# Query and key tiles turned by VectorE in 32x32 blocks instead of TensorE, in a two-layer streaming trunk

## The chip, the cores and the metric

The kernel runs on one NeuronCore of a Trainium2 chip. The metric is the device time of one execution in microseconds (us), median over the runs; lower is better. TensorE ran at its full granted clock in the profile of before.

## What is computed

`x` is 2048 tokens of 1024 channels. Layer A is a gated pooling mixer; layer B is stick-breaking attention with 16 heads of 64 channels against keys and values that are computed once from the output of layer A. The change lies where queries and keys are made:

```python
kv_in = rms_norm(x, kv_norm)
k_all, v_all = jnp.split(kv_in @ w_kv, 2, axis=-1)
k_sh = rms_norm(split_heads(k_all), k_norm)      # over the 64 channels of a head
v_sh = split_heads(v_all)
h = rms_norm(x, b_norm[j])
q, z = jnp.split(h @ b_w_in[j], 2, axis=-1)
q = rms_norm(split_heads(q), b_q_norm[j])
...
logits = jnp.einsum('bhtd,bhsd->bhts', q[:, :, t0:L], k[:, :, :L]) * SB_SCALE
```

The attention wants queries and keys with channels on the partitions; the norm over a head's channels is taken with tokens on the partitions. So each q and k tile has to be turned once.

## The kernel before

Every product is done in split precision: each operand is a pair (high part rounded to fp32r, low part the remainder), and three matmuls of 128x128 by 128x512 stand for one product.

The first half of the program, the dense stage, goes over four chunks `s` of 512 tokens. A chunk has 22 steps, written as a list: eight for the mixer (`run_z`, `run_u`), four for its output (`run_o`), four for the gate (`run_g`), and six token-major ones (`run_kvq`): q, k and v, each in two halves `b` of 512 channels (8 heads). A `run_kvq` step does two passes (`j0` = 0 and 2); a pass makes two tiles `j` of 128 tokens by 512 channels with 48 matmuls, in which the activations `ck["x2"]` (channels by tokens) are the stationary operand and the weights move. Tile `j` holds the tokens `128*j` to `128*j+127`.

For q and k, ScalarE takes a tile out of PSUM and scales it by the token's rsqrt (`keyed`: `qs`, then its square), VectorE sums the squares per head, GpSimd makes the rsqrt `rq`, and VectorE multiplies (`normed`: `qn`). When all four tiles of a half are there, four closures `finish(m)`, one for each pair of heads, are put on the list `lag`. They are issued at the end of the next step's first pass, after its last matmul group:

```python
while j0 == 0 and kt == KT - 1 and lag:
    lag.pop(0)()
```

Each `finish(m)` has TensorE turn four 128x128 blocks into PSUM (`pst`, two buffers), ScalarE write the high part of `hl` and VectorE the low part (for q both times the joint gain `gqk`), and the SP queue store `hl` (512 KB) to DRAM as `qd` or `kd`. `hl` has four buffers of a kind (`t4`) that weight repacking and the v tiles use too.

Weights for the coming steps are fetched by the SP queue (`fetch`) and made into pairs by ScalarE and VectorE (`convert`, L148 and L149 for q, k, v). The SP queue issues in program order (`queue` pins it), and so do the matmul stream and the operations marked `keep_in_program_order`; the rest is placed by a scheduler when the program is built. Each engine then works through its own row of instructions in order.

The second half is the attention: 16 heads by 4 query chunks by the key chunks below, with the z projection and the whole output stage of layer B as filler between the tiles. It reads `qd`, `kd`, `vd` back from DRAM and uses the per-token rsqrt `r2s` once more in `gate_z`.

Of the kernel before, what the change touches and what calls it, by code (L numbers as in the profile page):

```python
# [9 lines left out]
F32 = mybir.dt.float32  # L10
# [5 lines left out]
P = 128  # L16
# [19 lines left out]
def trunk_kernel(ctx, tc, x, xt, pt0, wut, cols, heads, zin, grp, aout, agate, aple,  # L36
# [22 lines left out]
    gqk = cp.tile([P, 1], F32, name="gqk")  # L59
    r2all = cp.tile([P, NSUB, 4], F32, name="r2all")  # L60
    r2s = [r2all[:, s, :] for s in range(NSUB)]

# [4 lines left out]
    qd = [[dram.tile([P, 2, W5], F32, name=f"qd{s}_{m}") for m in range(NH // 2)] for s in range(NSUB)]  # L67
    kd = [[dram.tile([P, 2, W5], F32, name=f"kd{s}_{m}") for m in range(NH // 2)] for s in range(NSUB)]
    vd = [[dram.tile([8, P, 4, P], F32, name=f"vd{s}_{b}") for b in range(2)] for s in range(NSUB)]
    ve = [[dram.tile([4, W5], F32, name=f"ve{s}_{b}") for b in range(2)] for s in range(NSUB)]  # L70

    wod = [dram.tile([P, 2, 2, 4, P], F32, name=f"wod{o}") for o in range(KT)]
# [146 lines left out]
    with ExitStack() as st:  # L219
# [15 lines left out]
            return t2.tile([P, W5], F32, tag="tmp", name=nm, bufs=8)  # L235

        hp = st.enter_context(tc.tile_pool(name="hp", bufs=1))
        halo = [[hp.tile([P, HALO], F32, name=f"halo{o}_{i}") for i in range(2)] for o in range(KT)]
        for o in range(KT):
            V.memset(halo[o][0], 0.0)  # L240
# [251 lines left out]
        def run_u(s, g, wu):  # L492

            ck, win = chunk[s], WIN[g]
            pss2 = [dense(), dense()]
            product(pss2, wu or ck["wu"].pop(g), ck["x"], (0, P), None, second_beside(g - 1) if g and not s else ())
            if "z3" in ck:
                ck["rb"] = bcast(ck["r"], "x")
                gate_of(ck, g, ck.pop("z3"))
            for k in range(2):  # L500
                o = 2 * g + k
                ub = t2.tile([P, HALO + W5], F32, tag="ub", name="ub", bufs=2)
                G.tensor_copy(out=ub[:, 0:HALO], in_=halo[o][s % 2])
                V.tensor_tensor(out=ub[:, HALO:], in0=pss2[k], in1=ck["rb"], op=ALU.mult)
                G.tensor_copy(out=halo[o][(s + 1) % 2], in_=ub[:, W5 : W5 + HALO])
                cur, lo, sh = ub, 0, 1
                while sh < win:
                    nx = t2.tile([P, HALO + W5], F32, tag="us", name="us", bufs=2)
# [62 lines left out]
        def run_g(s, b, wg, wl):  # L571
# [21 lines left out]
            for k in range(2):  # L593
# [6 lines left out]
                    sq = na  # L600
                ck["acc"] = sq

        def run_kvq(s, kind, b, ws):
            ck = chunk[s]
            for j0 in (0, 2):
# [3 lines left out]
                pss2 = [dense(), dense()]  # L609
                for kt in range(KT):  # L610
                    for i in range(2):
                        tk = slice((j0 + i) * P, (j0 + i + 1) * P)
                        for xh, wh in ((0, 0), (1, 0), (0, 1)):
                            T.matmul(pss2[i], ck["x2"][kt][:, xh, tk], wst(ws, kt, wh, 0, W5),  # L614
                                     start=(kt == 0 and xh == 0 and wh == 0), stop=(kt == KT - 1 and wh == 1))
                    if kt == 2:
                        stored_late()
# [4 lines left out]
                if "r2" not in ck:  # L622
                    ps = turned()
                    for j in range(4):
                        T.matmul(ps[:, 0, j : j + 1], ck["acc"][:, j * P : (j + 1) * P], ones,
                                 start=True, stop=True)
                    ss = t2.tile([P, 4], F32, tag="ssx", name="ss2")
                    A.copy(out=ss, in_=ps[:, 0, 0:4])
                    rsqrt_mean(r2s[s], ss, D, t2, "x")
                    ck["r2"] = r2s[s]  # L630
                fins = [token_major(s, kind, b, j0 + i, pss2[i]) for i in range(2)]
                if kind == "v":
                    settle()
# [12 lines left out]
                    pass  # L646

        def token_major(s, kind, b, j, ps):
            tk = slice(j * P, (j + 1) * P)
            rj = chunk[s]["r2"][:, j : j + 1]  # L650
            ps8 = ps.rearrange("q (h d) -> q h d", d=HD)
            if kind == "v":

# [63 lines left out]
            return lambda: normed(s, kind, b, j, qs, rq)  # L717

        def normed(s, kind, b, j, qs, rq):
            qn = t2.tile([P, 8, HD], F32, tag="qn", name="qn", bufs=5)  # L720
            tc.keep_in_program_order(
                V.tensor_tensor(out=qn, in0=qs, in1=rq.unsqueeze(2).to_broadcast([P, 8, HD]), op=ALU.mult))
            rows = chunk[s].setdefault((kind, b), [])
            rows.append(qn)
            if j < 3:
                return

            def finish(m):
                pt = turned()
                for i in range(4):  # L730
                    ins = T.transpose(pt[:, i, :], rows[i][:, 2 * m : 2 * m + 2, :].rearrange("q h d -> q (h d)"), ident)  # L731
                    if i == 0:
                        tc.keep_in_program_order(ins)
                pt = pt.rearrange("q j t -> q (j t)")
                hl = t2.tile([P, 2, W5], F32R, tag="t4", name="hl", bufs=4)
                if kind == "k":
                    split(hl, pt, V)
                else:
                    A.activation(out=hl[:, 0], in_=pt, func=AF.Identity, scale=gqk)
                    V.scalar_tensor_tensor(out=hl[:, 1], in0=pt, scalar=gqk, in1=f(hl[:, 0]),  # L740
                                           op0=ALU.mult, op1=ALU.subtract)
                queue(out=(kd if kind == "k" else qd)[s][4 * b + m], in_=f(hl))

            for m in range(4):
                lag.append(lambda m=m: finish(m))

        def load_gains():
            nc.scalar.dma_start(out=gains, in_=cols[:, KT:])
            gs = t2.tile([P, 2], F32, tag="gs", name="gs", bufs=1)
            nc.scalar.dma_start(out=gs, in_=heads)  # L750
            return gs

        def join_gains(gs):
            V.scalar_tensor_tensor(out=gqk, in0=gs[:, 1:2], scalar=HD ** -0.5, in1=gs[:, 0:1],
                                   op0=ALU.mult, op1=ALU.mult)

        steps = []
# [582 lines left out]
```

## Time and profile before

| what | value |
|---|---|
| median of 3 runs | 2680.74 us (2680.23 to 2682.93) |
| span of the profiled execution | 2679.3 us, so 1.4 us of the median lie around it if it ran as the median did |
| TensorE matmuls | busy 2668.1 us, 13358 instructions |
| VectorE, ScalarE, GpSimd busy | 1911.5, 1397.2 and 927.7 us |
| DMA | 590.00 MB, mean 220 GB/s |
| first and last matmul of the q, k, v steps (L614) | 219.8 and 1332.6 us |

Busy times are per engine and overlap. PE is the matmul row of TensorE, PEld its weight-load row, which runs beside it: the stationary operand of a matmul is loaded while the matmul before it streams. A matmul's recorded duration is longer than the distance to the next one, because matmuls are pipelined.

### The profile page before, as it was taken

What the parts mean: (1) busy time and instruction counts of PE and PEld (TensorE: products, weight loads), DVE (VectorE), ACT (ScalarE), POOL (GpSimd) and SP (SyncE); (2) the same over time, 40 slices, a digit from 0 to 9 for tenths busy, and PEclk for the clock granted to TensorE, in tenths of its full rate; (3) what the DMA queues carried; (4) which work ended last, traced back from release to release, by engine and by line L of the source; (5) the groups of instructions that cost most, each with busy time, mean ns of one, the idle gap of its engine ahead of it and who ended that gap; (6) DMA issues with size and microseconds to landing.
All of it is one profiled execution on the core that took longest, in us unless ns stands there. A gap on an engine that the chain in (4) does not pass through costs nothing.

```text
span 2679.3 us, 39424 instructions
## 1 busy us (share of the span) xinstructions
PE 2668.1 (100%) x13358; PEld 2229.9 (83%) x13358; DVE 1911.5 (71%) x2474; ACT 1397.2 (52%) x2735; POOL 927.7 (35%) x740
## 2 busy tenths in 40 slices
PE   9999999999999999999999999999999999999999
PEld 7888888888888888888888888888888888888887
DVE  6776625665266643665399999999999998886632
ACT  6455623455135551345356666666666666665531
POOL 2675337643486434853221111122111221212220
PEclk9999999999999999999999999999999999999999
DMA  8657795567856678543679665556766677778975
GB/s 327 222 175 271 251 308 188 192 240 251 303 175 226 232 259 298 168 151 134 223 236 286 195 220 176 166 172 191 211 199 177 185 222 227 201 209 261 267 237 177
DMA packets 281366, 590.00 MB, mean 220 GB/s; under 512 B 33702, under 2 KB 67750, under 8 KB 281164
## 3 DMA queue, kind: packets, MB, share of 16 engines
q1 hardware_dynamic: 270818, 571.41, 65.3%
q0 software_dynamic: 4608, 8.39, 1.9%
q10 hardware_dynamic: 5738, 7.68, 1.0%
q8 instruction: 106, 1.74, 0.3%
q14 instruction: 96, 0.79, 0.1%
HBM read 438.40 MB, written 136.38 MB: 215 GB/s over the span
## 4 chain that ended last, share of the span: by engine, by line
PE 97%; DVE 1%; DMA 0%; issue 0%; ACT 0%; SPq 0%; ACTq 0%; DVEq 0%
PE psd L614 19%; PE psd L168 9%; PE psd L167 9%; PE psd L166 9%; PE psa L961 9%; PE psd L1023 6%; PE psd L1025 6%; PE psd L1027 6%; PE pso L974 5%; PE psl L937 5%; PE pso L973 5%; PE psl L936 5%; PE pst L731 1%; PE psdt L1023 1%; PE psdt L1025 1%; PE psdt L1027 1%
## 5 line engine op out<-in xcount | busy, mean ns | idle before, releaser
L614 PE MATMUL psd<-wpair,x 128*128 128x512 f32 x2304 | 536.8, 391 | 0.0
L948 DVE TENSOR_TENSOR_SCAN pp<-kap,pp,zeros 128x512 f32<-128x512 f32 x384 | 513.5, 1339 | 7.7 <-ACT kap L940 7.0
L964 ACT CAST at<-psa 128x512 fp32r<-128x512 f32 (+3 forms) x640 | 325.7, 523 | 348.6 <-PE psa L961 338.1
L614 PEld LDWEIGHTS psd<-wpair,x 128*128 128x128 f32 x2304 | 429.9, 188 | 87.0
L965 DVE TENSOR_TENSOR at<-psa,at 128x512 fp32r<-128x512 f32 (+3 forms) x640 | 375.1, 598 | 62.0 <-ACT at L964 57.5
L940 ACT ACTIVATE kap<-psl 128x512 f32<-128x512 f32 (+3 forms) x640 | 345.7, 540 | 94.0 <-PE psl L937 90.6
L961 PE MATMUL psa<-ident,pp 128*128 128x128 f32 x2176 | 329.4, 273 | 2.0 <-DVE at L965 1.5
L961 PEld LDWEIGHTS psa<-ident,pp 128*128 128x128 f32 x2176 | 263.6, 140 | 58.2 <-DVE at L965 4.2
L936 PE MATMUL psl<-kk,qa 128*128 128x512 f32 (+3 forms) x640 | 275.1, 430 | 0.5 <-ACT at L964 0.5
L945 DVE TENSOR_TENSOR_SCAN pp<-kap,ahead 128x128 f32<-128x128 f32 (+3 forms) x256 | 224.3, 878 | 40.1 <-ACT kap L940 38.7
L974 PE MATMUL pso<-at,vv 128*128 128x512 f32 (+3 forms) x640 | 234.0, 366 | 0.0
L937 PE MATMUL psl<-kk,qb 128*128 128x512 f32 (+3 forms) x640 | 232.9, 364 | 0.0
L973 PE MATMUL pso<-at,vv 128*128 128x512 f32 (+3 forms) x640 | 232.3, 363 | 0.0
L167 PE MATMUL psd<-xp,wpair 128*128 128x512 f32 x512 | 199.5, 390 | 2.0 <-DVE xp L316 2.0
L166 PE MATMUL psd<-xp,wpair 128*128 128x512 f32 x512 | 199.8, 391 | 1.1 <-ACT xp L315 1.1
L168 PE MATMUL psd<-xp,wpair 128*128 128x512 f32 x512 | 199.3, 390 | 0.0
L149 DVE SCALAR_TENSOR_TENSOR wpair<-wraw,gains,wpair 128x512 fp32r<-128x512 f32 x192 | 161.7, 883 | 46.1 <-ACT wpair L148 45.6
L143 POOL TENSOR_TENSOR wpair<-wraw,wpair 128x512 fp32r<-128x512 f32 x99 | 145.5, 1479 | 82.0 <-ACT wpair L141 78.1
L148 ACT ACTIVATE wpair<-wraw,gains 128x512 fp32r<-128x512 f32 x192 | 132.9, 718 | 64.2 <-DMA wraw<-in_bq_dram 25.9
L141 ACT CAST wpair<-wraw 128x512 fp32r<-128x512 f32 x148 | 89.9, 618 | 121.4 <-PE psd L168 87.5
L1062 POOL TENSOR_TENSOR zr<-zr,sgz 128x512 f32<-128x512 f32 x32 | 61.6, 1924 | 257.3 <-ACT sgz L1061 233.8
L974 PEld LDWEIGHTS pso<-at,vv 128*128 128x128 f32 x640 | 120.2, 188 | 26.3
(207 smaller groups left out, 5338.9 us busy)
## 6 DMA issues: line engine op xcount, KB each, us to landing
kk<-kd SPq DMA_DIRECT2D x320, 128.0 KB
vv<-vd SPq DMA_DIRECT2D x160, 256.0 KB
wraw<-in_kv_dram SPq DMA_DIRECT2D x128, 256.0 KB
wpair<-wzd SPq DMA_DIRECT2D x64, 512.0 KB
wpair<-wod SPq DMA_DIRECT2D x64, 512.0 KB
wpair<-wgd SPq DMA_DIRECT2D x64, 512.0 KB
wpair<-wu SPq DMA_DIRECT2D x48, 512.0 KB
wpair<-wi SPq DMA_DIRECT2D x36, 512.0 KB
```

The costliest lines, as they stand in the source:

```text
L166: T.matmul(ps, wst(units, kt, 0, c0), acts[kt][:, 0], start=(begin and kt == order[0]), stop=False)
L167: T.matmul(ps, wst(units, kt, 0, c0), acts[kt][:, 1], start=False, stop=False)
L168: T.matmul(ps, wst(units, kt, 1, c0), acts[kt][:, 0], start=False, stop=(end and kt == order[-1]))
L614: T.matmul(pss2[i], ck["x2"][kt][:, xh, tk], wst(ws, kt, wh, 0, W5), start=(kt == 0 and xh == 0 and wh == 0), stop=(kt == KT - 1 and wh == 1))
L936: T.matmul(ps[:, :w], qa[:, qs], kk[:, :w], start=True, stop=False)
L937: T.matmul(ps[:, :w], qb[:, qs], kk[:, :w], start=False, stop=True)
L940: A.activation(out=kp[:, r0:], in_=ps[:, :w], func=AF.Sigmoid, scale=-1.0)
L948: V.tensor_tensor_scan(out=pp[:, ::-1], data0=kp[:, ::-1], data1=zeros.to_broadcast([P, W5]), initial=st["carry"][j], op0=ALU.mult, op1=AL ...
L961: T.transpose(pt[:, j * P : (j + 1) * P], pp[:, r0 + kt * P : r0 + (kt + 1) * P], ident)
L965: V.tensor_tensor(out=at[:, 1, cs], in0=pt[:, cs], in1=f(at[:, 0, cs]), op=ALU.subtract)
L973: T.matmul(po[:, cs], vv[:, kt, :], at[:, 0, cs], start=(st["diag"] and kt == 0), stop=False)
L974: T.matmul(po[:, cs], vv[:, kt, :], at[:, 1, cs], start=False, stop=(st["last"] and kt == 3))
```

## The change

A q or k tile `j` now holds every fourth token of the chunk (tokens `4*t + j`), by taking the stationary operand with a step of four elements (`tokens`); the sum of squares for the per-token rsqrt is taken the same way. `normed` multiplies in place (`qs`), and VectorE turns the 16 blocks of 32 channels by 32 tokens of a tile in each of the four quarters of the partitions, writing into one shared tile `blocks` with a step of four elements, so that after four tiles the tokens of a quarter stand in order. `finish(m)` no longer uses TensorE or PSUM: it reads `blocks`; for q it takes two operations of 256 elements on each engine, since the gain now differs by 32-channel half. The store of `hl` becomes four DMAs, one for each 32 partitions, which put the blocks in place in `qd` or `kd` in runs of 512 bytes; what lies in DRAM afterwards is the same. `blocks` lies over the tile `work` that now also holds the pooling sums of `run_u` (`ub`, `us` before). Since v and `gate_z` keep the old order of tokens, the per-token rsqrt goes through DRAM once (`r2d`) and is read back in that order as `r2s`.

```diff
+        work = hp.tile([P, 4, HALO + W5], F32, name="work")
+        blocks = work.rearrange("q e n -> q (e n)")[:, 0 : 4 * W5].rearrange("q (g t j) -> q g t j", j=4, t=32)
...
-                ub = t2.tile([P, HALO + W5], F32, tag="ub", name="ub", bufs=2)
+                ub = work[:, k]
...
+        def tokens(ap, kind, j):
+            if kind == "v":
+                return ap[:, j * P : (j + 1) * P]
+            return ap.rearrange("q (t j) -> q t j", j=4)[:, :, j]
...
-                            T.matmul(pss2[i], ck["x2"][kt][:, xh, tk], wst(ws, kt, wh, 0, W5),
+                            T.matmul(pss2[i], tokens(ck["x2"][kt][:, xh], kind, j0 + i), wst(ws, kt, wh, 0, W5),
...
-                    rsqrt_mean(r2s[s], ss, D, t2, "x")
-                    ck["r2"] = r2s[s]
+                    r2 = ck["r2"] = t2.tile([P, 4], F32, tag="r2", name="r2", bufs=1)
+                    rsqrt_mean(r2, ss, D, t2, "x")
+                    pend.append(lambda: queue(out=r2d[s].rearrange("a (t j) -> (a t) j", j=4), in_=r2))
+                if kind == "k" and b == 0 and j0 == 0:
+                    queue(out=r2s[s], in_=r2d[s].rearrange("j t -> t j"))
...
-                V.tensor_tensor(out=qn, in0=qs, in1=rq.unsqueeze(2).to_broadcast([P, 8, HD]), op=ALU.mult))
+                V.tensor_tensor(out=qs, in0=qs, in1=rq.unsqueeze(2).to_broadcast([P, 8, HD]), op=ALU.mult))
+            tc.keep_in_program_order(
+                V.transpose(out=blocks[:, :, :, j], in_=qs.rearrange("q h (g t) -> q (h g) t", t=32)))
...
-                pt = turned()
-                for i in range(4):
-                    ins = T.transpose(pt[:, i, :], rows[i][:, 2 * m : 2 * m + 2, :].rearrange("q h d -> q (h d)"), ident)
...
-                    split(hl, pt, V)
+                    split(hl, src, V)
                 else:
-                    A.activation(out=hl[:, 0], in_=pt, func=AF.Identity, scale=gqk)
-                    V.scalar_tensor_tensor(out=hl[:, 1], in0=pt, scalar=gqk, in1=f(hl[:, 0]),
-                                           op0=ALU.mult, op1=ALU.subtract)
-                queue(out=(kd if kind == "k" else qd)[s][4 * b + m], in_=f(hl))
+                    for e in range(2):
+                        part = lambda ap: ap.rearrange("q (g e t) -> q g e t", e=2, t=P)[:, :, e, :]
+                        A.activation(out=part(hl[:, 0]), in_=part(src), func=AF.Identity, scale=gqk[:, e : e + 1])
+                        V.scalar_tensor_tensor(out=part(hl[:, 1]), in0=part(src), scalar=gqk[:, e : e + 1],
+                                               in1=part(f(hl[:, 0])), op0=ALU.mult, op1=ALU.subtract)
+                dst = (kd if kind == "k" else qd)[s][4 * b + m].rearrange("(g t) l n -> t l g n", t=32)
+                for a in range(4):
+                    queue(out=dst[:, :, :, a * P : (a + 1) * P],
+                          in_=f(hl)[a * 32 : a * 32 + 32].rearrange("q l (g n) -> q l g n", n=P))
```

How the rows move, shown at the first chunk. TensorE, at the end of the first pass of the second q step; `pst` is the PSUM tile of the transposes, `x_...` the activation pairs. Before:

```order
L614 MATMUL psd<-wpair,x_2486 128x512 x6
L614 MATMUL psd<-wpair,x_2489 128x512 x6
L731 MATMUL pst<-ident,qn 128x128 x8
L614 MATMUL psd<-wpair,x_2070 128x512 x6
L731 MATMUL pst<-ident,qn 128x128 x4
L614 MATMUL psd<-wpair,x_2073 128x512
L731 MATMUL pst<-ident,qn 128x128 x4
L614 MATMUL psd<-wpair,x_2073 128x512 x5
```

The same place now:

```order
L623 MATMUL psd<-wpair,x_2463 128x512 x6
L623 MATMUL psd<-wpair,x_2466 128x512 x6
L623 MATMUL psd<-wpair,x_2047 128x512 x6
L623 MATMUL psd<-wpair,x_2050 128x512 x6
L623 MATMUL psd<-wpair,x_2182 128x512 x6
```

The sixteen transposes that stood between the two passes are gone; nothing else on TensorE changed place.

VectorE, from the second pass of the first q step to the first pass of the second; `ssq` is the sum of squares, `wpair<-wraw` a weight conversion for the coming step. Before:

```order
L714 TENSOR_REDUCE ssq<-sqq 128x8
L722 TENSOR_TENSOR qn<-qs,rq 128x512 x2
L714 TENSOR_REDUCE ssq<-sqq 128x8
L740 SCALAR_TENSOR_TENSOR hl<-pst,gqk,hl 128x512 x2
L149 SCALAR_TENSOR_TENSOR wpair<-wraw,gains,wpair 128x512
L740 SCALAR_TENSOR_TENSOR hl<-pst,gqk,hl 128x512 x2
L714 TENSOR_REDUCE ssq<-sqq 128x8
L722 TENSOR_TENSOR qn<-qs,rq 128x512 x2
```

Now:

```order
L725 TENSOR_REDUCE ssq<-sqq 128x8
L732 TENSOR_TENSOR qs<-qs,rq 128x512
L734 STREAM_TRANSPOSE work<-qs 128x512
L732 TENSOR_TENSOR qs<-qs,rq 128x512
L734 STREAM_TRANSPOSE work<-qs 128x512
L747 SCALAR_TENSOR_TENSOR hl<-work,gqk,hl 128x2x128 x8
L725 TENSOR_REDUCE ssq<-sqq 128x8 x2
L732 TENSOR_TENSOR qs<-qs,rq 128x512
```

Each multiplication is now followed by a block transpose, and the four operations of 512 elements that took the turned blocks out of PSUM are eight of 256 from SBUF.

The SP queue, behind the finish of the first q half. Before:

```order
L90 DMA qd_0_192<-hl 128x1024
L90 DMA qd_1_193<-hl 128x1024
L90 DMA qd_2_194<-hl 128x1024
L90 DMA qd_3_195<-hl 128x1024
L90 DMA xin<-in_xt_dram 128x512 x2
L90 DMA xn<-in_x_dram 128x1024
L90 DMA wraw<-in_kv_dram 128x512 x8
```

Now:

```order
L91 DMA qd_0_192<-hl 64x4x128 x4
L91 DMA qd_1_193<-hl 64x4x128 x4
L91 DMA qd_2_194<-hl 64x4x128 x4
L91 DMA qd_3_195<-hl 64x4x128 x4
L91 DMA xin<-in_xt_dram 128x512 x2
L91 DMA xn<-in_x_dram 128x1024
L91 DMA wraw<-in_kv_dram 128x512 x8
```

Four stores became sixteen, ahead of the same loads.

More of the change, by code (lines that the diff above doesn't have):

```diff
@@ L58, in trunk_kernel @@
     g_s, g_b, g_kv = (gains[:, i * KT : (i + 1) * KT] for i in range(3))
-    gqk = cp.tile([P, 1], F32, name="gqk")
+    gqk = cp.tile([P, 2], F32, name="gqk")
     r2all = cp.tile([P, NSUB, 4], F32, name="r2all")
@@ L69, in trunk_kernel @@
     vd = [[dram.tile([8, P, 4, P], F32, name=f"vd{s}_{b}") for b in range(2)] for s in range(NSUB)]
+    r2d = [dram.tile([4, P], F32, name=f"r2d{s}") for s in range(NSUB)]
     ve = [[dram.tile([4, W5], F32, name=f"ve{s}_{b}") for b in range(2)] for s in range(NSUB)]
@@ L505, in run_u @@
                 G.tensor_copy(out=halo[o][(s + 1) % 2], in_=ub[:, W5 : W5 + HALO])
-                cur, lo, sh = ub, 0, 1
+                cur, lo, sh, turns = ub, 0, 1, 0
                 while sh < win:
-                    nx = t2.tile([P, HALO + W5], F32, tag="us", name="us", bufs=2)
+                    nx = work[:, 2 + turns % 2]
+                    turns += 1
                     lo += sh
@@ L624, in run_kvq @@
                     for j in range(4):
-                        T.matmul(ps[:, 0, j : j + 1], ck["acc"][:, j * P : (j + 1) * P], ones,
+                        T.matmul(ps[:, 0, j : j + 1], tokens(ck["acc"], "q", j), ones,
                                  start=True, stop=True)
@@ L648, in token_major @@
         def token_major(s, kind, b, j, ps):
-            tk = slice(j * P, (j + 1) * P)
-            rj = chunk[s]["r2"][:, j : j + 1]
+            rj = (r2s[s] if kind == "v" else chunk[s]["r2"])[:, j : j + 1]
             ps8 = ps.rearrange("q (h d) -> q h d", d=HD)
@@ L719, in normed @@
         def normed(s, kind, b, j, qs, rq):
-            qn = t2.tile([P, 8, HD], F32, tag="qn", name="qn", bufs=5)
             tc.keep_in_program_order(
-                V.tensor_tensor(out=qn, in0=qs, in1=rq.unsqueeze(2).to_broadcast([P, 8, HD]), op=ALU.mult))
-            rows = chunk[s].setdefault((kind, b), [])
-            rows.append(qn)
+                V.tensor_tensor(out=qs, in0=qs, in1=rq.unsqueeze(2).to_broadcast([P, 8, HD]), op=ALU.mult))
+            tc.keep_in_program_order(
+                V.transpose(out=blocks[:, :, :, j], in_=qs.rearrange("q h (g t) -> q (h g) t", t=32)))
             if j < 3:
@@ L728, in finish @@
             def finish(m):
[L729 to L734 removed]
                 hl = t2.tile([P, 2, W5], F32R, tag="t4", name="hl", bufs=4)
+                src = blocks[:, 4 * m : 4 * m + 4].rearrange("q g t j -> q (g t j)")
                 if kind == "k":
[L737 removed]
+                    split(hl, src, V)
                 else:
[L739 to L742 removed]
+                    for e in range(2):
[7 more added lines that the diff above has]
+                          in_=f(hl)[a * 32 : a * 32 + 32].rearrange("q l (g n) -> q l g n", n=P))
             for m in range(4):
@@ L748, in load_gains @@
             nc.scalar.dma_start(out=gains, in_=cols[:, KT:])
-            gs = t2.tile([P, 2], F32, tag="gs", name="gs", bufs=1)
+            gs = t2.tile([P, 4], F32, tag="gs", name="gs", bufs=1)
             nc.scalar.dma_start(out=gs, in_=heads)
@@ L753, in join_gains @@
         def join_gains(gs):
-            V.scalar_tensor_tensor(out=gqk, in0=gs[:, 1:2], scalar=HD ** -0.5, in1=gs[:, 0:1],
+            V.scalar_tensor_tensor(out=gqk, in0=gs[:, 2:4], scalar=HD ** -0.5, in1=gs[:, 0:2],
                                    op0=ALU.mult, op1=ALU.mult)
@@ L1314 @@
                                  columns(given["kv_norm"])], axis=1),
-        "heads": _np.stack([_np.tile(given["k_norm"], 2), _np.tile(given["b_q_norm"][0], 2)], axis=1),
+        "heads": _np.tile(_np.concatenate([given["k_norm"].reshape(2, 32), given["b_q_norm"][0].reshape(2, 32)]).T, (4, 1)),
         "zin": packed(given["a_w_in"][0], 256, 2),
```

1 line of the change is left out of this document (removed).

## The prediction

> **What bounds the kernel now.** I read the page's busy shares and the shares of its chain first, to learn which engine sets the end.
>
> ```profile
> span 2679.3 us, 39424 instructions
> PE 2668.1 (100%) x13358; PEld 2229.9 (83%) x13358; DVE 1911.5 (71%) x2474; ACT 1397.2 (52%) x2735; POOL 927.7 (35%) x740
> ...
> PE 97%; DVE 1%; DMA 0%; issue 0%; ACT 0%; SPq 0%; ACTq 0%; DVEq 0%
> ```
>
> TensorE is busy throughout and the chain runs on it for 97%. So what leaves TensorE's row leaves the time, as long as the others keep up with the shorter row. Next I read the chain in order of time where the change lies, the q and k steps of the first chunk (start, length, what).
>
> ```profile
> 256.94 20.19 PE psd L614 x89
> 277.14 0.87 PE pst L731 x8
> 278.01 1.40 PE psd L614 x6
> 279.40 0.53 PE pst L731 x4
> 279.93 0.24 PE psd L614
> 280.17 0.44 PE pst L731 x4
> 280.61 20.19 PE psd L614 x89
> ```
>
> The matmuls of L614 follow each other at 20.19 / 89 = 0.227 us. One group of sixteen transposes takes 0.87 + 0.53 + 0.44 = 1.84 us of the chain, all of it TensorE's own time. The groups by tile `qn` give the count and the waits ahead of them:
>
> ```profile
> L731 PE MATMUL pst<-ident,qn x256: 270/272/331, 253.3 to 1301.6; 128*128 128x128 f32 x128
> ...
>   DVE hl L740: 2.5, 8
>   DVE hl L256: 1.9, 4
> ```
>
> 256 transposes are 16 such groups; their waits for a free `pst` buffer are 4.4 us and lie within the lengths above.
>
> **What leaves.** 16 groups x 1.84 us = 29.4 us of TensorE's row. The sum is made against the profiled execution, 2679.3 us, which is 1.4 us below the median, so 29.4 off the median gives 2651.3.
>
> **What could come back on TensorE: the stepped weight load.** For q and k, 16 steps of 96 matmuls, 1536 loads of the stationary operand now step by four elements. No row shows such a load, so it is bounded. How much room a load has is seen where narrow matmuls leave loads back to back, beside the loads of L614:
>
> ```profile
> 1397.43 0.19 PEld L936 LDWEIGHTS psl<-kk,qa 128*128 128x128 f32 x1
> 1397.54 0.19 PEld L937 LDWEIGHTS psl<-kk,qb 128*128 128x128 f32 x1
> 1397.65 0.19 PEld L973 LDWEIGHTS pso<-at,vv 128*128 128x128 f32 x1
> ...
> 257.93 14.24 PEld L614 LDWEIGHTS psd<-wpair,x 128*128 128x128 f32 x63
> ```
>
> Loads can follow each other at 0.11 us although each is recorded as 0.19; under L614 one is due only every 14.24 / 63 = 0.226 us. So a load may become twice as long and cost nothing, since the matmul before it hides it. Lower end: nothing, for a gain is excluded where the matmul of 512 columns sets the pace. Upper end: the load passes over all 512 elements at its own pace, 4 x 0.11 = 0.44 us, which is 0.213 over the matmul and 327 us over 1536. I take nothing, by the nearest row of a walk over the same bytes: the moving operand of the same matmul passes 512 elements of each partition in 0.227 us, and the stepped load covers just such a stretch, so at the moving side's pace it ends with the matmul. This is an estimate with almost no room to spare, and it is the main doubt. The gain is used up when the load exceeds the matmul by 29.4 us / 1536 = 19 ns, at about 0.246 us, 2.2 times the unit-step load.
>
> [...] No run here shows a stepped load yet.
>
> **What VectorE gets.** Per chunk 16 block transposes (64 in all), and the finishes read SBUF instead of PSUM.
>
> ```profile
> L714 DVE TENSOR_REDUCE ssq<-sqq x64: 672/685/689, 234.6 to 1290.7; 128x8 f32<-128x512 f32 x64
> L948 DVE TENSOR_TENSOR_SCAN pp<-kap,pp,zeros x384: 1252/1275/2677, 1341.5 to 2401.4; 128x512 f32<-128x512 f32 x192
> L740 DVE SCALAR_TENSOR_TENSOR hl<-pst,gqk,hl x32: 739/742/747, 254.8 to 1255.4; 128x512 fp32r<-128x512 f32 x32
> L149 DVE SCALAR_TENSOR_TENSOR wpair<-wraw,g_a,wpair x24: 470/475/1567, 27.4 to 90.5; 128x256 fp32r<-128x256 f32 x24
> L256 DVE TENSOR_TENSOR hl<-pst,hl x32: 680/682/692, 302.1 to 1302.5; 128x512 fp32r<-128x512 f32 x32
> L256 DVE TENSOR_TENSOR x<-tx,x x32: 678/693/1789, 182.1 to 1196.9; 128x512 fp32r<-128x512 f32 x32
> ```
>
> Columns are minimum, median and maximum in ns. A transpose of 512 elements lies between a plain pass (0.68) and the slowest kind of pass here (the scan, 1.28); I take 1.2, near the scan, because its output is stepped. A q finish goes from 4 x 0.742 to 8 x 0.475, +0.8 us. A k finish keeps its four operations, but with both inputs in SBUF: between nothing and 4 x (1.789 - 0.682) = 4.4 us, as the `x<-tx` row spreads; I take 1. The stages of the first chunk, q, k and v in this order:
>
> ```profile
> core 0: us, PE busy (x) PEld busy (x) DVE busy (x) ACT busy (x) POOL busy (x), PEclk, DMA share, GB/s
> 219.80:266.10 46.30, 46.30 (x218) 38.46 (x217) 30.55 (x43) 25.25 (x45) 22.06 (x19) 1.00 0.67 240
> 266.10:313.60 47.50, 47.46 (x226) 39.19 (x225) 31.25 (x49) 30.36 (x54) 17.20 (x17) 1.00 0.73 264
> 313.60:358.90 45.30, 45.30 (x209) 37.66 (x208) 18.13 (x26) 19.81 (x34) 12.61 (x11) 1.00 0.77 250
> ```
>
> The q window holds one finish and shrinks by 1.84 us to 44.5; the k window holds two and shrinks to 43.8. VectorE then has, in q, 30.6 + 8 x 1.2 + 0.8 = 41.0 of 44.5 us (36.8 to 41.6 over the bounds), and in k, 31.3 + 9.6 + 0.8 + 1 = 42.7 of 43.8 (37.5 to 46.7). That fits, barely; v, with 18 of 43.5, takes up a backlog. What stands behind a late VectorE is the next step's weight conversions, which TensorE needs, and the `qs` buffers that ScalarE's next evictions need. ScalarE: a q finish goes from four operations to eight; even at an unchanged 0.69 us each (the 512-element `hl` activation) that is 2.7 us more, on 30.4 of 43.8. I add 2 us for places where TensorE catches up with a conversion: 2653.
>
> ```profile
> L739 ACT ACTIVATE hl<-pst,gqk x32: 671/686/706, 254.1 to 1254.5; 128x512 fp32r<-128x512 f32 x32
> ...
> L90 SPq DMA_DIRECT2D qd<-hl x32: 319/320/327, 255.6 to 1256.2; - x32
> L90 SPq DMA_DIRECT2D vd<-vv x32: 359/371/772, 336.3 to 1386.5; - x32
> ...
> SPq L90 <- DVE hl L740: 24.5, 8, 11.6
> SPq L90 <- DVE hl L256: 22.8, 8, 9.6
> ```
>
> **The SP queue and the DMA engines.** A finish issues 16 stores in place of 4: 12 more at 0.32 to 0.37 us, up to 4.4 us of the SP queue, ahead of the `xin`, `xn` and `wraw` loads behind it. Those weights are for the step after the next, 22 us on, and the queue already waits 24.5 us over eight stores for `hl` (mean 3, up to 11.6) in these windows with no harm to TensorE. So: nothing; if that cover were gone, 4.4 us for each of the 16 finishes, 70 us. The `vd` stores, already in 512-byte runs, say what such bytes cost: in the v window 0.77 of the engines move 250 GB/s, in k 0.73 move 264. I put the sixteen stores of a q or k window at 10 points of share more, 0.83 at most; hidden. `r2d` is stored in the first q step, read back in the first k step, and first used by v two steps, 44 us, later; hidden. `work` keeps two buffers for each of the two pooling sums, and its last reader as `blocks` comes a step before `run_u`; nothing. The attention reads the same bytes; nothing.
>
> **The rivals.**
> First, slower: the stepped load outgrows its matmul. For it: each load sits against a cover that ends at 0.227 us; against it: the moving operand's pace above. At the middle of the bounds, 0.275 us, it costs 48 ns x 1536 = 74 us: 2653 + 74 = 2727. It decides from 0.246 us on.
> Second, VectorE becomes the bound of the k windows: at its upper end 46.7 us of work meet 43.8 us of matmuls, 2.9 us late in each chunk, and as much again in the weight conversions queued behind it and in ScalarE's waits: 8 x 2 = 16 us at most, 14 more than I put in: 2667. For it speaks 97% occupancy at my values; against it, v's idle half.
> Third, the change brings nothing because something else sets the end of the dense stage: 2681. Against it, the chain is 97% TensorE's own work, and the 29.4 us are a part of that.
>
> **How the numbers follow.** The forecast as told 0.58, its own range 2645 (all of TensorE's groups, some reload time and no stall) to 2662; the second rival 0.12 (2662 to 2675, still faster); the third 0.06; the first 0.24, of which a third lies above 2740. So the range is 2645 to 2740, leaving out about one in ten on the long side and little below. A measurement of this kernel can tell 0.2%, 5.4 us, from no change: faster 0.69, same 0.07, slower 0.24.
>
> **What would show it.** The L731 group is gone. The L614 matmuls of q and k keep 0.227 us from one to the next while their recorded loads grow from 0.19 to about 0.3 us; if the distance is over 0.23 beside unstepped v matmuls at 0.227, the first rival is at work. VectorE's transposes read 1.0 to 1.4 us and its busy time in the k window is 40 to 44 us; a TensorE wait there for `wpair` shows the second. Wrong would be also a wait of TensorE on PSUM behind ScalarE's `hl` casts in the v steps, which now stand ahead of evictions and wait for stores to free a buffer.

## The result and the profile after

The changed kernel is slower: 2811.8 us median (2809.9 to 2812.6) against 2681.0 (2680.2 to 2682.9), ratio 1.0485, 95% interval 1.0473 to 1.0498. The forecast was 2653, the range 2645 to 2740. First the page's busy shares and its chain, the counterpart of the first lines of before.

```profile
span 2809.7 us, 39253 instructions
PE 2686.9 (96%) x13102; PEld 2297.8 (82%) x13102; DVE 1970.4 (70%) x2570; ACT 1404.1 (50%) x2767; POOL 928.4 (33%) x740
PEclk9999989999899998999999999999999999999999
PE 90%; DMA 3%; DVE 2%; issue 2%; ACT 1%; SPq 0%; ACTq 0%; POOL 0%; DVEq 0%; POOLq 0%
```

TensorE has 256 matmuls fewer and is no longer busy throughout; 10% of the chain runs elsewhere, and there are three dips in its granted clock where before was at full clock throughout. What TensorE waits for, from the first q step to the last v step (us in all, times, longest):

```profile
PE psd L623 <- ACT wpair L149: 59.9, 8, 11.6
PE psd L167 <- DMA wpair<-wz: 43.1, 3, 14.9
```

103 us in eleven waits, all for weights. The windows of the first chunk show where: q (two steps), k (two), v (two, the second up to the first matmul of the next chunk).

```profile
core 0: us, PE busy (x) PEld busy (x) DVE busy (x) ACT busy (x) POOL busy (x), PEclk, DMA share, GB/s
220.30:244.70 24.40, 24.40 (x106) 24.40 (x106) 17.86 (x24) 14.45 (x26) 11.82 (x11) 1.00 0.87 298
244.70:267.30 22.60, 22.60 (x98) 22.60 (x98) 17.47 (x27) 11.77 (x24) 10.40 (x9) 1.00 0.52 128
267.30:289.80 22.50, 22.50 (x98) 22.50 (x97) 15.41 (x23) 12.16 (x23) 9.81 (x9) 1.00 0.80 249
289.80:318.10 28.30, 22.75 (x98) 22.43 (x97) 17.71 (x30) 15.16 (x31) 12.07 (x12) 0.98 0.73 208
318.10:354.60 36.50, 24.86 (x97) 19.66 (x97) 15.30 (x23) 12.86 (x22) 7.31 (x8) 0.83 0.45 122
354.60:393.10 38.50, 23.61 (x97) 19.03 (x97) 12.12 (x18) 14.11 (x23) 6.83 (x6) 0.81 0.73 199
```

The first three steps run without a wait, though the two q steps take 47.0 us where 44.5 were forecast. Then TensorE waits before the first v step, before the second, and before the next chunk, 6, 12 and 15 us, and no engine is near full there: VectorE has 15 of 36 us, the DMA engines move 122 GB/s at a share of 0.45. So nothing is short of capacity; something stands in line. The SP queue's row over these steps says what (start, length, what):

```profile
278.05 21.98 SPq L91 DMA_DIRECT2D qd<-hl  x16
302.26 5.50 SPq L91 DMA_DIRECT2D wraw<-in_kv_dram  x8
309.51 31.95 SPq L91 DMA_DIRECT2D kd<-hl  x16
347.57 6.68 SPq L91 DMA_DIRECT2D wraw<-in_kv_dram  x8
354.82 20.87 SPq L91 DMA_DIRECT2D kd<-hl  x16
387.89 2.22 SPq L91 DMA_DIRECT2D wpair<-wz  x4
```

Sixteen stores of a finish occupy the queue for 21 to 32 us, and the weights stand behind them. In the first row, the q finish, 10 us are issues and as much again is one wait for `hl`. What the queue waited for there, and the third and fourth cast of that finish, which the scheduler that fills ScalarE's row put behind weight conversions and an eviction:

```profile
SPq L91 <- DVE hl L747: 10.8, 2, 10.2
292.84 1.69 ACT L746 ACTIVATE hl<-work,gqk 128x256 fp32r<-128x256 f32 x4
```

The first k finish before, at the same place, has four stores:

```profile
302.85 3.73 SPq L90 DMA_DIRECT2D kd<-hl  x4
308.89 5.38 SPq L90 DMA_DIRECT2D wraw<-in_kv_dram  x8
```

Most of the 32 us of the first k finish is one wait. Between 318.3 and 337.0 us the queue got three stores out; first its row, then what it waited for there:

```profile
318.33 18.70 SPq L91 DMA_DIRECT2D kd<-hl  x3
```

```profile
SPq L91 <- DMA vs<-vr: 16.9, 1, 16.9
```

And what the DMA engines did from 309 to 345 us (40 slices of 0.9 us, busy tenths):

```profile
DMA  9999999189935000000000000000811999669606
```

The first of the three stores had just taken a quarter of the same `hl`, so the data of the second was there. It waited 16.9 us for `vs<-vr`, a copy that ScalarE issues for a v tile, of which it uses nothing, and meanwhile the DMA engines stood still for fifteen slices. The built program explains the tie: in it each transfer of the SP queue and of ScalarE's queue is counted by one of eight counters, dealt out in turn, and a transfer waits for the one that had its counter before. These are the rows of the SP queue for that `hl`, with what they wait for; `DVE` is VectorE's half of the tile, the others are four of the eight counters:

```
L91 DMA kd_2_226<-hl 64x4x128 [waits DMAHW6_49,DVE_49]
L91 DMA kd_2_226<-hl 64x4x128 [waits DMAHW1_49]
L91 DMA kd_2_226<-hl 64x4x128 [waits DMAHW2_49]
L91 DMA kd_2_226<-hl 64x4x128 [waits DMAHW3_49]
```

The transfer that had `DMAHW1` before the second store is ScalarE's `vs<-vr`. Four stores of a finish use four counters; sixteen go round all eight twice, with ScalarE's copies for v among them. ScalarE can issue that copy only when it has taken the v tile out of PSUM, which TensorE had to make first (from 318.1 us on). TensorE's next weights stood behind the store. So TensorE waited, in the end, for a store that waited for TensorE's own later work.

After each wait the clock is lower. Windows of the wait for `wz` and of the 7 us behind it:

```profile
378.00:393.00 15.00, 0.14 (x1) 0.00 (x1) 4.67 (x7) 6.15 (x11) 4.24 (x4) 0.63 0.79 221
393.00:400.00 7.00, 6.97 (x19) 5.52 (x20) 0.12 (x1) 0.62 (x1) 0.00 (x0) 0.58 1.07 354
```

Two matmuls of the chain in the second window:

```profile
393.79 0.43 PE psd L168
394.64 0.43 PE psd L167
```

0.43 us a matmul where it is 0.227 at full clock. Finer windows of the same stretch:

```profile
377.80:381.80 4.00, 0.34 (x2) 0.00 (x0) 0.69 (x1) 1.69 (x3) 0.14 (x1) 0.99 0.30 90
381.80:393.00 11.20, 0.00 (x0) 0.00 (x1) 3.97 (x6) 4.66 (x8) 4.10 (x4) 0.50 0.96 267
393.00:398.80 5.80, 5.77 (x14) 4.54 (x15) 0.00 (x0) 0.00 (x0) 0.00 (x0) 0.50 1.05 355
398.80:400.00 1.20, 1.20 (x7) 0.98 (x6) 0.12 (x1) 0.62 (x1) 0.00 (x0) 0.99 1.15 347
```

The granted clock is 0.50 from 381.8 us, 4 us after the start of TensorE's last matmul before the wait (377.8), to 398.8, 6 us after the first matmul behind it (393.0).

### The profile page after: what moved, and what is told of

The parts are those of the page before. It is cut to its first block, busy times and chain, and to the rows that moved or that the text cites. A ratio compares the mean times of both kernels' runs of the same rounds, so it can differ in the third digit from the quotient of the medians.

```text
span 2809.7 us, 39253 instructions
## 1 busy us (share of the span) xinstructions
PE 2686.9 (96%) x13102; PEld 2297.8 (82%) x13102; DVE 1970.4 (70%) x2570; ACT 1404.1 (50%) x2767; POOL 928.4 (33%) x740
## 4 chain that ended last, share of the span: by engine, by line
PE 90%; DMA 3%; DVE 2%; issue 2%; ACT 1%; SPq 0%; ACTq 0%; POOL 0%; DVEq 0%; POOLq 0%
PE psd L623 18%; PE psd L167 9%; PE psd L168 9%; PE psd L169 9%; PE psa L971 8%; PE psd L1033 6%; PE psd L1035 6%; PE psd L1037 6%; PE pso L984 4%; PE psl L947 4%; PE pso L983 4%; PE psl L946 4%; PE psdt L1033 1%; PE psdt L1035 1%; PE psdt L1037 1%
## 5 line engine op out<-in xcount | busy, mean ns | idle before, releaser
L623 PE MATMUL psd<-wpair,x 128*128 128x512 f32 x2304 | 557.1, 404 | 60.1 <-ACT wpair L149 59.9
L623 PEld LDWEIGHTS psd<-wpair,x 128*128 128x128 f32 x2304 | 516.4, 274 | 99.1 <-ACT wpair L149 62.9
L955 DVE TENSOR_TENSOR_SCAN pp<-kap,ahead 128x128 f32<-128x128 f32 (+3 forms) x256 | 222.9, 873 | 41.2 <-ACT kap L950 35.6
L167 PE MATMUL psd<-xp,wpair 128*128 128x512 f32 x512 | 203.0, 397 | 43.7 <-DMA wpair<-wz 43.1
L168 PE MATMUL psd<-xp,wpair 128*128 128x512 f32 x512 | 201.9, 395 | 1.8 <-DVE xp L319 1.8
L169 PE MATMUL psd<-xp,wpair 128*128 128x512 f32 x512 | 201.3, 393 | 0.0
L167 PEld LDWEIGHTS psd<-xp,wpair 128*128 128x128 f32 x512 | 97.5, 191 | 65.9 <-issue 44.3
```

The costliest lines, as they stand in the source:

```text
L167: T.matmul(ps, wst(units, kt, 0, c0), acts[kt][:, 0], start=(begin and kt == order[0]), stop=False)
L168: T.matmul(ps, wst(units, kt, 0, c0), acts[kt][:, 1], start=False, stop=False)
L169: T.matmul(ps, wst(units, kt, 1, c0), acts[kt][:, 0], start=False, stop=(end and kt == order[-1]))
L623: T.matmul(pss2[i], tokens(ck["x2"][kt][:, xh], kind, j0 + i), wst(ws, kt, wh, 0, W5), start=(kt == 0 and xh == 0 and wh == 0), stop=(kt = ...
```

## Experiments

Theory A: the sixteen stores of a finish make the weights behind them on the SP queue late. Theory B: VectorE's turns and the shared tile put ScalarE's casts, evictions and weight conversions out of step. Theory C: the stepped weight load, and the clock that falls with it. Ratios are to the kernel before, run again beside each (2680.6 to 2681.3 us). Each kernel is scheduled anew when it is built, so an edit can also move rows that it doesn't name.

**Which part of the change.** Four kernels, each with one part done or undone.

The stores alone, on the kernel before (queries and keys land scrambled):

```diff
-                queue(out=(kd if kind == "k" else qd)[s][4 * b + m], in_=f(hl))
+                dst = (kd if kind == "k" else qd)[s][4 * b + m].rearrange("(g t) l n -> t l g n", t=32)
+                for a in range(4):
+                    queue(out=dst[:, :, :, a * P : (a + 1) * P],
+                          in_=f(hl)[a * 32 : a * 32 + 32].rearrange("q l (g n) -> q l g n", n=P))
```

> The kernel before with nothing changed but the stores: each q and k tile pair leaves as four stores of 32 partitions in 512-byte runs, to the addresses of the changed kernel (so the queries and keys that land are scrambled; transposes stay on TensorE, loads are unit-step). Theory A (the sixteen stores of a finish hold the SP queue for 20 us or more ahead of the weight loads): the three waits of a chunk on late weights come back, 90 to 130 us slower than before, 2770 to 2810. Theory B (VectorE's transposes and the shared tile put casts, evictions and conversions out of step): within 10 us of before. Theory C (the stepped weight load, and the clock that falls with it): no change, 2681.

2834.3 us, ratio 1.057 (1.0555 to 1.0586): 154 slower, more than the whole change, which has its gain from the transposes to set against it. TensorE's waits are the same three in each chunk (46.1 us on `wpair`, 43.2 on `wz`); its transposes wait 15.3 us more for a free `pst`. A holds, and its price was put too low by 20 us and more.

The changed kernel with one store for each tile pair (the blocks then stand in the wrong places):

```diff
-                dst = (kd if kind == "k" else qd)[s][4 * b + m].rearrange("(g t) l n -> t l g n", t=32)
-                for a in range(4):
-                    queue(out=dst[:, :, :, a * P : (a + 1) * P],
-                          in_=f(hl)[a * 32 : a * 32 + 32].rearrange("q l (g n) -> q l g n", n=P))
+                queue(out=(kd if kind == "k" else qd)[s][4 * b + m], in_=f(hl))
```

> The changed kernel, with each tile pair leaving as one store of 128 partitions in 4 KB rows as before (its blocks then stand in the wrong places; everything else as changed). A: the waits on weights vanish, 2655 to 2690: the 29 us of transposes are gained less the stepped loads' price. B: still 2790 to 2812. C: still 2790 to 2812.

2699.1 us, 1.0067 (1.005 to 1.0084). The same kernel once more, in a single execution:

> A second look at the kernel of the second experiment: 2697 to 2701.

2701.1. 113 us of the loss go, but not all: before stays ahead by 18. Of TensorE's waits one kind of any size is left, at the start of each chunk:

```profile
PE psd L167 <- DMA wpair<-wu: 22.1, 3, 7.9
PE psd L623 <- ACT wpair L149: 3.1, 3, 1.2
```

The stepped load alone, on the kernel before:

```diff
-                            T.matmul(pss2[i], ck["x2"][kt][:, xh, tk], wst(ws, kt, wh, 0, W5),
+                            T.matmul(pss2[i], tokens(ck["x2"][kt][:, xh], kind, j0 + i), wst(ws, kt, wh, 0, W5),
```

> The kernel before with nothing changed but the stationary operand of the q and k matmuls, taken with a step of four elements (tokens come out in another order). A and B: the load is hidden but for the 5 to 9 ns a matmul that the changed kernel's trace shows between matmuls without a wait, 0.236 for 0.227 us over 1536: 2681 to 2697. C: 60 us or more slower, 2740 to 2810.

2696.6 us, 1.0059 (1.0044 to 1.0074): 16 us, 10 ns for each of 1536 loads. One row of its chain against the same stretch of before, which follows it:

```profile
232.81 22.79 PE psd L619 x96
```

```profile
231.59 21.88 PE psd L614 x96
```

0.237 against 0.228 us. C is not the loss, but it is a price.

The changed kernel with the same stores issued later, behind the loads:

```diff
-                    queue(out=dst[:, :, :, a * P : (a + 1) * P],
-                          in_=f(hl)[a * 32 : a * 32 + 32].rearrange("q l (g n) -> q l g n", n=P))
+                    pend.append(lambda a=a: queue(out=dst[:, :, :, a * P : (a + 1) * P],
+                          in_=f(hl)[a * 32 : a * 32 + 32].rearrange("q l (g n) -> q l g n", n=P)))
```

> The changed kernel with the same sixteen stores of a finish, issued at the third matmul group of the next pass, so that on the SP queue the activation and weight loads come ahead of them. A: most of the 106 us of TensorE's waits goes, 2670 to 2730. B and C: as the changed kernel, 2790 to 2815, or longer where casts wait for the stores to free their buffers.

2767.0 us, 1.0324 (1.0308 to 1.0339), outside what any theory said. The waits before the v steps are gone and stand at the next chunk's start instead; TensorE's two largest:

```profile
PE psd L167 <- DMA wpair<-wz: 61.7, 3, 21.8
PE psl L946 <- DMA kk<-kd: 9.3, 1, 9.3
```

Putting the stores behind one group of loads puts them ahead of the next.

**What about the stores: number, shape or length.** The kernel before again, with whole 4 KB rows, so that the layout stays right and the number alone is changed: four stores a tile pair of 32 partitions, three (48, 40, 40), or two of 64, which makes sixteen, twelve, eight a finish. The first of them:

```diff
-                queue(out=(kd if kind == "k" else qd)[s][4 * b + m], in_=f(hl))
+                dst = (kd if kind == "k" else qd)[s][4 * b + m]
+                for a in range(4):
+                    queue(out=dst[a * 32 : a * 32 + 32], in_=f(hl)[a * 32 : a * 32 + 32])
```

> The kernel before with each tile pair stored as four stores of 32 partitions whose 4 KB rows stay whole; layout and sums as before. It has the sixteen stores of a finish, without the 512-byte runs. If the length of an issue counts (0.61 us for a scattered store, 0.32 for a whole one, so 10 us of the SP queue against 5), about half of the first experiment's 154 us is left, 2740 to 2770. If the number of stores counts, because each store waits for an earlier transfer on another queue, nearly all is left, 2800 to 2835. If the 512-byte runs themselves count, 2681 to 2690.

> The kernel before with two stores of 64 partitions for each tile pair, 4 KB rows whole: eight stores a finish, one for each of the eight counters, where the fifth experiment had sixteen and before four. If the loss follows the number, a third of it (four more of twelve more stores): 2720 to 2745. If it begins only where a finish wraps around the eight counters, under 10 us: 2681 to 2691.

> The kernel before with three stores for each tile pair (48, 40 and 40 partitions, 4 KB rows whole): twelve a finish, between the twelfth experiment's eight that cost nothing and the fifth's sixteen that cost 155 us. If the loss sets in as soon as a finish goes more than once round the eight counters: 2730 to 2800. If it sets in only when the SP queue runs out of time: 2681 to 2710.

The last column is the SP queue's waits for ScalarE's copies (`vs`, `ve`) from 219 to 1460 us.

| stores a finish | median us | ratio (interval) | waits for copies, us |
|---|---|---|---|
| 4 (before) | 2681 | 1 | 20 |
| 8 | 2682.6 | 1.0004 (0.9995 to 1.0014) | 57 |
| 12 | 2752.8 | 1.0265 (1.0251 to 1.0279) | 126 |
| 16 | 2835.8 | 1.058 (1.0562 to 1.0597) | 189 |

The 512-byte runs cost nothing by themselves: sixteen stores of whole rows (e5_quart, 2835.8 us) lose as much as sixteen scattered ones (e1_stores, 2834.3). Nor is it the length of an issue. First the issues of the eight, then of the twelve, then of the sixteen (ns, minimum, median, maximum):

```profile
L90 SPq DMA_DIRECT2D qd<-hl x64: 445/596/1670, 255.5 to 1260.8; - x64
```

```profile
L90 SPq DMA_DIRECT2D qd<-hl x96: 292/351/1447, 256.6 to 1317.0; - x96
```

```profile
L90 SPq DMA_DIRECT2D qd<-hl x128: 302/420/1852, 255.1 to 1384.0; - x128
```

8 x 0.596 = 4.8 us of the queue cost nothing, 12 x 0.351 = 4.2 us cost 72, and 16 x 0.420 = 6.7 us cost 155. Twelve stores that take the queue less time than eight lose; in these runs once round the eight counters is free and the loss begins beyond. The first chunk's v window at eight and at sixteen, the eight first:

```profile
313.00:355.00 42.00, 42.00 (x195) 34.87 (x194) 18.90 (x27) 18.62 (x31) 10.16 (x8) 1.00 0.88 264
```

```profile
313.00:355.00 42.00, 27.93 (x116) 21.89 (x116) 13.46 (x21) 14.37 (x25) 7.22 (x7) 0.84 0.28 83
```

From eight on, the more stores, the idler the DMA engines: a share of 0.88 at eight, 0.51 at twelve, 0.28 at sixteen.

**The shared counters.** The changed kernel with ScalarE's copies for v issued by GpSimd, whose transfers have eight counters of their own in the built program; the sixteen stores stay on SP.

```diff
-                start = nc.sync.dma_start if last else nc.scalar.dma_start
+                start = nc.sync.dma_start if last else nc.gpsimd.dma_start
```

> The changed kernel, stores as it has them on the SP queue, but the small shift copies of the v tiles (vs and ve) issued by GpSimd instead of ScalarE, whose transfers are counted by other counters than those that the SP queue and ScalarE share. Theory A1 (a store waits for one of eight shared counters, and so for a ScalarE copy that can't run before TensorE has got further): SP's 115 us of waits on vs and 42 us on ve vanish, and TensorE's waits fall by half or more, 2690 to 2760. A2 (the stores are slow by themselves or hold the four t4 buffers too long): 2780 to 2815.

2758.0 us, 1.0284 (1.0269 to 1.0299). SP's 115 and 42 us of waits on `vs` and `ve` are gone, the waits at the next chunk's start shrink to 7 us, and 54 of the 131 us come back. 77 stay. Sixteen stores still take 16 x 0.61 = 10 us to issue, and the first q finish still holds the queue for 22 us, with the same wait of 10.2 us for `hl`. They also go twice round counters that the queue's own loads use, but that doesn't show as waits: the queue's list names no store of `qd` or `kd`, and its waits for its own weights are shorter than before's (`wraw` 11.4 us for 14.4, `wu` 5.6 for 15.6). So the 77 are put down to the issues and the late casts, which no run takes apart. ScalarE's row, too, was relieved of the issues, so not all of the 54 need be the counters.

The sixteen stores on GpSimd instead; and that with the finishes written after the evictions of the pass, which brings ScalarE's v evictions ahead of the last key casts:

```diff
-                    queue(out=dst[:, :, :, a * P : (a + 1) * P],
+                    G.dma_start(out=dst[:, :, :, a * P : (a + 1) * P],
...
-                    while j0 == 0 and kt == KT - 1 and lag:
-                        lag.pop(0)()
...
                 fins = [token_major(s, kind, b, j0 + i, pss2[i]) for i in range(2)]
+                while j0 == 0 and lag:
+                    lag.pop(0)()
```

> The changed kernel, with the sixteen stores of a finish issued by GpSimd instead of SP (GpSimd then has its own row of instructions to keep up with, 22 of 46 us busy in a q window before). Theory A (SP queue): the weight loads are on time again and the waits go, 2655 to 2700. Theory B (VectorE and ScalarE out of step): 2790 to 2815. If GpSimd takes over 1 us for an issue, the per-head rsqrt behind it is late and the time stays above 2750.

> As the sixth, with the finishes written after the evictions of the pass they stand in, which puts ScalarE's value evictions ahead of the last key finish's casts in its row. A: as the sixth, at most 30 us less: 2655 to 2690. B: half or more of the loss goes by the order alone.

2748.5 us (1.025, 1.0235 to 1.0265) and 2738.5 (1.0214, 1.0199 to 1.0229). The waits inside the v steps go, 51 to 56 us at the next chunk's start stay, and the order is worth 10 us. I had expected everything back; the v stores still stood on the SP queue ahead of `wz`.

**What is left at the next chunk's start.** The kernel of one store with the evictions of v pinned ahead of the key casts:

```diff
-                A.activation(out=vr, in_=ps8, func=AF.Identity, scale=rj)
+                tc.keep_in_program_order(A.activation(out=vr, in_=ps8, func=AF.Identity, scale=rj))
...
-                    split(hl, src, V)
+                    ins = A.copy(out=hl[:, 0], in_=src)
+                    if b:
+                        tc.keep_in_program_order(ins)
+                    V.tensor_tensor(out=hl[:, 1], in0=src, in1=f(hl[:, 0]), op=ALU.subtract)
```

(with the finishes after the evictions, as above)

> The kernel of the second experiment (one store for each tile pair, blocks in wrong places), with ScalarE's evictions of the first v tiles pinned ahead of the four casts of the last key finish. If those casts, waiting for VectorE's last transposes, are what makes the v tiles, their stores and the weights behind them late, TensorE's 22 us of waits at the next chunk's start and the clock lost with them go: 2664 to 2680. If not, 2694 to 2702.

2691.8 us, 1.0043 (1.0027 to 1.006): between the two answers. TensorE's wait on `wu` falls from 22.1 to 10.3 us. The order that B names is worth 7 us, no more.

The v stores moved to GpSimd too, in the seventh kernel:

```diff
-                stay(queue(
+                stay((queue if last else G.dma_start)(
                     out=vd[s][b][:, :, j, :].rearrange("h q n -> q h n"), in_=f(vv).rearrange("q h e d -> q h (e d)")))
```

> As the seventh (q and k stores issued by GpSimd, finishes written after evictions), with the v stores moved to GpSimd as well, so that only loads stand ahead of the next chunk's weights on the SP queue. If it is the row of the SP queue that makes them late, TensorE's 51 us of waits there go: 2665 to 2700. If it is v itself, late for want of a t4 buffer that the stores still hold, 2720 to 2745.

2683.9 us, 1.0009 (1.0 to 1.0019). No wait for weights is left in the dense stage, whose last q, k, v matmul starts at 1319.2 us (before 1332.6). The 13 us are lost again where the attention begins; two windows of its first 30 us:

```profile
1319.20:1334.20 15.00, 13.81 (x66) 11.22 (x64) 2.04 (x4) 4.64 (x10) 6.23 (x9) 1.00 1.01 336
1334.20:1349.20 15.00, 10.49 (x37) 7.37 (x38) 12.62 (x16) 6.62 (x14) 2.45 (x2) 0.77 0.61 203
```

VectorE has 2.0 us of work in the first 15. Its first scan of the attention waits 9.0 us, until the last of GpSimd's v stores has landed (the mask that GpSimd makes behind its stores was ready before, at 1330.7 us); two pieces of the chain:

```profile
1328.93 7.34 DMA vd<-vv
1336.59 2.97 DVE pp L955 x4
```

This run also warns against adding up waits: the SP queue still waits 60.5 and 35.6 us on `vs` and `ve` there, up to 25.8 us at a time, and it costs TensorE nothing. In the first chunk the weights of the v steps had been issued ahead of the longest wait, and the next chunk's, behind it, still came in time.

**A version that beats both.** Three ways of sharing the stores out, all with the finishes after the evictions:

```diff
+                    (queue if a < 2 else G.dma_start)(out=dst[:, :, :, a * P : (a + 1) * P],
...
+                stay((queue if s == NSUB - 1 else G.dma_start)(
                     out=vd[s][b][:, :, j, :].rearrange("h q n -> q h n"), in_=f(vv).rearrange("q h e d -> q h (e d)")))
```

The first line alone is e13_mix, both are e14_mix_vd; e15_last_mix has the second and, for the first, `a < 2 and s == NSUB - 1`.

> The changed kernel with finishes written after evictions (as in the seventh) and the sixteen stores of a finish shared out: two of each four on SP, two on GpSimd. A1 (shared counters; eight SP stores of a finish go once round them): the waits of the q, k and v steps go; 2665 to 2700 if the next chunk's start is in time too, 2720 to 2745 if it is still held by the v stores as in the seventh. A2 (a store of 32 partitions is slow wherever it is issued): above 2735.

> As e13_mix, with the v stores on GpSimd in the first three chunks. If the v stores ahead of the next chunk's weights on the SP queue are what is left in the seventh: 2664 to 2680, that is before less 29 for the transposes and plus 16 for the stepped loads.

> As e11_pool_vd in the first three chunks (all stores of q, k and v on GpSimd); in the last chunk the q and k stores shared between SP and GpSimd and the v stores on SP. If GpSimd's stores of the last chunk, ahead of what GpSimd prepares for the attention, cost the 15 us that the eleventh loses there: 2666 to 2675. If not, 2680 to 2686.

2690.8 us (1.0037, 1.0023 to 1.0051), **2666.8** (0.9949, 0.9936 to 0.9961) and 2667.3 (0.9948, 0.9935 to 0.996). All three take back 121 us and more of the loss, and the last two are 14 us faster than before, clear of the spread. With eight stores of a finish on SP the q, k and v steps run without a wait (A), so a store of 32 partitions isn't slow by itself; the v stores on SP hold the next chunk's weights (15.1 us of waits on `wu`, 24 us of time); and the 15 us that e11_pool_vd lost at the attention's start were GpSimd's last stores, which e15_last_mix shares out. In e14_mix_vd the q, k and v steps of a chunk are one piece of the chain but for the sums of squares:

```profile
223.34 11.28 PE psd L623 x48
236.26 122.73 PE psd L623 x528
```

## Why the prediction was wrong, step by step

- **What bounds the kernel, and what leaves**: right. The transposes are 29.4 us of the path, and e14_mix_vd shows that they can be had. It is 14 us faster, about 29.4 less 12 for the stepped loads (8 ns each in that run: 11.28 / 48 = 0.235 us a matmul) and 3.4 for the sums of squares below.
- **The stepped load**, "I take nothing": mis-sized, 16 us (10 ns each in e3_step). The sums of squares, whose matmuls have one column, have their loads close behind each other: the eight matmuls, stepped and, in before, unit-step, then six of their loads in the same order.

```profile
231.67 1.63 PE pst L634 x8
```

```profile
230.81 0.79 PE pst L625 x8
```

```profile
231.72 1.50 PEld L634 LDWEIGHTS pst<-ones,acc 128*128 128x128 f32 x6
```

```profile
230.75 0.75 PEld L625 LDWEIGHTS pst<-ones,acc 128*128 128x128 f32 x6
```

  One load is recorded as 0.33 us there, in before as 0.19, so they follow each other at (1.50 - 0.33) / 5 = 0.234 us against (0.75 - 0.19) / 5 = 0.112. That is not under a matmul of 0.227, as the forecast had it, but 7 ns over, and the q and k matmuls follow each other at 0.235 in the changed kernel (36.44 us for 155, from 252.8 us on), at 0.237 in e3_step. By the forecast's own sign, a distance over 0.23, the first rival is at work with 0.237, but at a fifth of its price: its 0.275 and 74 us did not come. The sums of squares themselves, 0.84 us more in each chunk, 3.4 in all, were left out.
- **VectorE**: right. Its groups of the changed kernel (ns, minimum, median, maximum):

```profile
L734 DVE STREAM_TRANSPOSE work<-qs x64: 1056/1106/1124, 240.3 to 1404.6; 128x512 f32<-128x512 f32 x64
L747 DVE SCALAR_TENSOR_TENSOR hl<-work,gqk,hl x64: 475/482/486, 254.8 to 1360.6; 128x256 fp32r<-128x256 f32 x64
L259 DVE TENSOR_TENSOR hl<-work,hl x32: 675/688/721, 305.3 to 1423.7; 128x512 fp32r<-128x512 f32 x32
```

  A transpose takes 1.106 us for the 1.2 forecast, a q finish's operation of 256 elements 482 ns for 475, a k finish's 688 for 682, so the 1 us put in there wasn't needed. VectorE has 95.9 us in the six windows of the first chunk against 79.9 before, where 22 more were forecast for q and k, and part of it moved into v. The second rival didn't come, although its sign did, a wait of TensorE for `wpair` at the end of the k steps: VectorE has 17.7 of 28.3 us there, and the weights were late on the SP queue.
- **The SP queue and the DMA engines**: this step failed. It priced the twelve more stores by the length of their issue (4.4 us a finish, at most 70) and then took nothing. The issue was 0.61 us rather than 0.32 to 0.37. The same sum with 0.61 gives 16 x 8.5 = 136 us, near the loss, but by luck: for e12_half it gives 16 x 3.5 = 56 us where 2 were lost, and e5_quart loses as much as e1_stores at 0.42. Not priced was what a store may wait for. It counted the queue's waits for `hl` in the first chunk, and before had other rows in the same list, here for all four chunks:

```profile
SPq L90 <- DMA ve<-vr: 12.1, 3, 5.0
SPq L90 <- DMA vs<-vr: 8.3, 3, 3.3
```

  A queue that waits for a copy with which it shares no data is tied to the other queue by something else; 20 us in before, 157 now. "Those weights are for the step after the next, 22 us on" was the cover, and a wait of 16.9 us in the middle of 16 stores uses it up. And though the text had a price of 70 us for the cover gone, no rival and no chance went with it: the 0.24 for slower was the stepped load's alone.
- **The DMA share**, 0.83 at most: no limit. It was 0.87 in the fullest step, which has no wait, and 0.45 in the worst.
- **The attention gets the same bytes, nothing**: its start lost 14 us (from the last q, k, v matmul to the last matmul of all 1356.5 us for 1342.5). Where no queue was behind, in e15_last_mix, nothing was lost there.
- **What would show it**: the casts of `hl` ahead of v's evictions were named, as a wait of TensorE on PSUM. That wait isn't in its list; the order makes v late instead, worth 7 us in e10_one_pin.

The account of the profiled execution, 130.4 us longer: -29.4 for the transposes, 13 (1536 x 8 ns, at 0.235 us a matmul) and 3.4 for the loads, 103 of named waits, 14 at the attention's start, 104 together; the remaining 26 are the lower clock. With each of the eleven waits the trace has a stretch of 3.4 to 17.1 us at a granted clock of 0.50, and the 116 matmuls that start in these stretches follow each other at 0.44 us, 51.0 us where 0.2275 each would make 26.4: 24.6 us more, so the parts add up to within 2.

What stays open: how much of the loss at sixteen stores is the tie to ScalarE's copies and how much the ten us of issues, the late casts of `hl` and the queue's own second round; e9_vspool removes the tie and gains 54 of 131 us, and e13_mix, which halves the number on SP and with it all of these, is clean in the q, k and v steps.

## What to carry to other kernels

When a change multiplies the transfers on a queue, don't price them by their issue: here 12 x 0.351 us cost 72 us and 8 x 0.596 cost 2. Count how often they go round the counters they share, and look for which other queue's transfers stand in between and what those wait for. The sign here was a queue's waits for transfers of which it uses nothing, 20 us in the profile before and 157 after, and beside the full queue DMA engines that stood still for fifteen slices of 0.9 us; the built program says which counter ties them. Then share the stores out over queues with counters of their own (14 us gained in e14_mix_vd), and look at what each of those queues has behind them (13 us lost where the attention begins in e11_pool_vd).

## What the runs showed of the hardware

- Loads of a stationary operand of 128x128 with a step of four fp32 elements follow each other at 0.234 us under matmuls of one column (changed kernel), at unit step at 0.112 (before). Under matmuls of 512 columns, which follow each other at 0.227 us with unit-step loads (before), the step costs 8 ns a matmul (changed kernel, 0.235) and 10 ns (e3_step, 0.237).
- On the SP queue a store of 32 partitions takes 0.61 us to issue (medians) in 512-byte runs (changed kernel) and 0.37 to 0.42 with whole 4 KB rows (e5_quart); one of 64 partitions 0.59 to 0.60 (e12_half), one of all 128 partitions 0.32 (before). GpSimd's issue of the scattered one takes 0.61 (e14_mix_vd).
- VectorE turns 128x512 fp32 in 32x32 blocks, with its output stepped by four elements, in 1.106 us (changed kernel).
